# Layer 0's gate product on two float16 parts, with scales taken from the squares of the loaded tiles

## The chip, the cores and the metric

The kernel runs on one core of a Trainium2 chip. The metric is the device time of one execution in microseconds (us). Three runs of the kernel before gave 1795.43 to 1798.64 us, with a median of 1796.76 us.

## The reference

A two-layer transformer block on 256 tokens of width 2048, with a context of 256 more tokens; the widths inside are 4096. Only layer 0, the Fourier branch, matters here. Its input is normalised, scaled and shifted, and its weight matrix gives two halves: `u`, which goes through a Fourier transform and a small mixing product, and `z`, which gates the result.

```python
h = _rmsnorm(x, norm_g[i]) * (1 + scale) + shift      # x and context: 512 columns together
u, z = jnp.split(h @ w_in, 2, axis=-1)                # w_in: 2048 x 8192
...                                                   # u -> Fourier transform, mixing -> f
return f * jax.nn.silu(z)
```

Everything is in float32, and the kernel reaches that accuracy by cutting each operand into a rounded high part and a remainder, with three products for one: high by high, high by low, low by high.

## The kernel before, in words

The program is written as tiles and operations; a planner orders the instructions of each engine by a simulated timeline, by readiness first and by their order in the program after that, and places the waits. `issue_after` lets the author put one instruction behind another on its engine. A pool with a tag holds a fixed number of buffers, and a load waits until one is free.

Layer 0 runs in this order:

- The opening: statistics, the conditioning vectors `gs0` (scale) and `sh0` (shift), and the transform of x.
- The U stage: a loop over 16 groups `g`. Each group loads two raw tiles of 1016 KB (`load_uh`), folds them into a minus part (line 133) and a plus part (line 139 for the first tile; for the second an accumulating DMA from GpSimd's queue, line 142), splits the parts on ScalarE and VectorE (lines 65 and 66) into eight buffers of the pool `wfp`, and multiplies: m-part, then the mixing product of the group before, then p-part. One group takes some 14.4 us in the trace. The raw tiles come from the pool `raw`, with three buffers; the pool `ws` has six of 4 KB.
- The gate stage. `make_hs(k)` makes the 16 moving operands of 128x512: `t = x * gs0 * r_bc` (line 716, VectorE), `h = t + sh0` on ScalarE (line 717), and the remainder on VectorE (line 718), into buffers `act`, of which there are 33. The first four output blocks share four weight tiles `wz0`, all 16 k for four blocks at once (lines 732 to 751). Each of the other 28 blocks (lines 752 to 761) loads one tile `wz` of 1 MB, splits it in two halves, and runs 16 x 3 matmuls of 512 columns (`mm3`, lines 78 to 80). `z_out` takes Silu from PSUM, multiplies it into `y`, and calls `next(ada)`: one piece of the conditioning product of later use, eight multiply-and-sum operations of 128x512 on VectorE (line 687) on another raw tile of 1 MB. There are 31 such pieces in these 28 blocks.
- The output product of layer 0 (lines 798 on) and layer 1 follow.

The weight tiles and the pieces of `ada` share the three raw buffers and the queue of SyncE (SP). Weights and moving operands of the gate product are of type float32r:

```python
    def half_split(t, i):
        h = wsp.tile([P, 1024], F32R, tag="ws", name="wh")
        l = wsp.tile([P, 1024], F32R, tag="ws", name="wl")
        split(h, l, t[:, i * 1024 : (i + 1) * 1024])
        return h, l
...
    us.close()
...
    adat = lay0.enter_context(tc.tile_pool(name="adat", bufs=1))
```

The pool `adat` is opened when the pools of the U stage (`wfp`, `ua`, `up`) have been closed, at the place in SBUF where they began. A pool that lands on a closed pool's bytes waits, by default, for every user of that pool.

Of the kernel before, what the change touches and what calls it, by code (L numbers as in the profile page):

```python
# [3 lines left out]

# [5 lines left out]

# [7 lines left out]
P = 128  # L18
# [13 lines left out]
def tile_dit(ctx: ExitStack, tc: tile.TileContext, a: dict, out: bass.AP):  # L32
# [18 lines left out]

    last_dma = [None]

    def act(dt=F32):
        return actp.tile([P, 512], dt, tag="act", name="act")

    def cload(name, shape, q=None, pool=const):
        t = pool.tile(shape, F32, tag=name, name=name)
# [94 lines left out]

    lay0 = ctx.enter_context(ExitStack())
    adap = lay0.enter_context(tc.tile_pool(name="ada", bufs=1))
    r_bc = adap.tile([P, 512], F32, name="r_bc")
    c32 = adap.tile([P, KT, 32], F32, name="c32")
    GP.memset(c32, 0.0)
# [513 lines left out]
    def ada_jobs():  # L672
        for pieces in ((0,), (1, 2, 3)):
            for kh in range(2):
                cb = adap.tile([P, 2, 1024], F32, tag="cb", name="cb")
                with tc.issue_after(hs_end[2]):
                    nc.gpsimd.dma_start(cb, a["crow"][:, kh].broadcast_to([P, 2, 1024]))
                with tc.issue_after(hs_end[1]):
                    S.activation(cb, cb, AF.Silu)
                for i in pieces:  # L680
                    for fg in range(8):
                        w = raw(a["adw"][i, kh, fg])
# [17 lines left out]
    with tc.tile_pool(name="yp", reuse_waits="tile", bufs=32) as ypool:  # L700
# [4 lines left out]
        hs = []  # L705
        hs_end = [None] * 3

        def make_hs(k):
            xt = act()
            hs_end[2] = nc.gpsimd.dma_start(xt, a["xT"][:, k, :]).ins  # L710
            h, l = act(F32R), act(F32R)
            for s in range(2):
                q = slice(s * N, (s + 1) * N)
                t = xt[:, q]
                with tc.issue_after(ft_end[1]):
                    V.scalar_tensor_tensor(t, t, gs0[:, k, s : s + 1], r_bc[:, q], op0=ALU.mult, op1=ALU.mult)
                hs_end[1] = S.activation(h[:, q], t, AF.Identity, bias=sh0[:, k, s : s + 1]).ins
                hs_end[0] = V.scalar_tensor_tensor(l[:, q], t, sh0[:, k, s : s + 1], h[:, q].bitcast(F32), op0=ALU.add, op1=ALU.subtract).ins
            hs.append((h, l))

        with tc.tile_pool(name="zp", reuse_waits="tile", bufs=2) as zp:
            def z_out(b, o):
                y = ys[b]
                z = zp.tile([P, 512], F32, tag="z", name="z")
                S.activation(z, o, AF.Silu)
                V.tensor_tensor(y, y, z, op=ALU.mult)
                if b >= 4:
                    with tc.issue_after(hs_end[0]) if b < 8 else nullcontext():
                        for _ in range(2 if b in (10, 17, 24) else 1):
                            next(ada)  # L730

            o4 = [psum() for _ in range(4)]
            for kg in range(4):
                wr = raw(a["wz0"][kg])
                w = []
                for i in range(2):
                    make_hs(kg * 4 + i * 2)
                    with tc.issue_after(hs_end[0]) if kg else nullcontext(), tc.issue_after(hs_end[1]) if kg else nullcontext():
                        w.append(half_split(wr, i))
                    make_hs(kg * 4 + i * 2 + 1)  # L740
                for j in range(4):
                    k = kg * 4 + j
                    wh, wl = w[j // 2]
                    for b in range(4):
                        q = slice((j % 2) * 512 + b * P, (j % 2) * 512 + (b + 1) * P)
                        mm3(o4[b], wh[:, q], wl[:, q], hs[k][0], hs[k][1], k == 0, k == KT - 1)
            for b in range(4):
                with tc.issue_after(last_dma[0]):
                    nc.sync.dma_start(ys[b], fd[b])
            for b in range(4):  # L750
                z_out(b, o4[b])
            for b in range(4, NB):
                w = ws_split(raw(a["wz"][b - 4]))
                with tc.issue_after(last_dma[0]):
                    nc.sync.dma_start(ys[b], fd[b])
                o = psum()
                for k in range(KT):
                    wh, wl = w[k // 8]
                    q = slice((k % 8) * P, (k % 8 + 1) * P)
                    mm3(o, wh[:, q], wl[:, q], hs[k][0], hs[k][1], k == 0, k == KT - 1)  # L760
                z_out(b, o)


        x1, sqs = [], []
# [689 lines left out]
```

## Time and profile before

| | |
|---|---|
| median of the runs | 1796.76 us (1795.43 to 1798.64) |
| the profiled execution | 1796.56 us, of which its span is 1794.8 us |
| TensorE (PE) busy | 1759.0 us, 98% of the span |
| VectorE (DVE) busy | 1410.7 us, 79% |
| ScalarE (ACT) busy | 899.5 us, 50% |
| GpSimd (POOL) busy | 211.5 us, 12% |
| granted TensorE clock | 0.998 |
| moved by DMA | 398.86 MB |

PE is the matmul stream and PEld the weight loads beside it. A matmul's duration includes its way through the array, so the rate of a stream is read from the starts of neighbours, not from the durations. An engine's idle time is put down to what ended it.

### The profile page before, as it was taken

The page shows a single profiled execution, that of the slowest core. Times are in us where ns is not written, and L with a number is a line of the kernel's source. Part 1 is how long each engine was busy: PE and PEld are TensorE (multiplying, and loading weights), DVE is VectorE, ACT ScalarE, POOL GpSimd, SP SyncE. Part 2 cuts the span into 40 slices and gives each one's busy share as a digit, 9 for nine tenths or more (in the row PEclk, how much of TensorE's full clock was granted, in tenths as well). Part 3 has the DMA queues.
Part 4 walks back from the last instruction along what each step waited for, and adds up shares of the span by engine and source line. Part 5 has one row for each costly group of instructions (what it writes and reads, how often), then busy time and mean ns, then how long its engine had stood idle before and what let it go on. Part 6 is the DMA issues. An engine that isn't in the chain of part 4 may idle for free. (4 is left out here: it accounts for less than half of the span.)

```text
span 1794.8 us, 26039 instructions
## 1 busy us (share of the span) xinstructions
PE 1759.0 (98%) x9449; PEld 1478.9 (82%) x9449; DVE 1410.7 (79%) x2761; ACT 899.5 (50%) x1543; POOL 211.5 (12%) x213
## 2 busy tenths in 40 slices
PE   6999999999999999999999999999999999999997
PEld 4679999888888888888888888878888888887886
DVE  5779889787879888775986473989999899998455
ACT  5545445432222243323322443678887888886343
POOL 0001112100000000000001000332212211233001
PEclk9999999999999999999999999999999999999999
DMA  9998888666666757662558332488898888887553
GB/s 394 417 344 231 235 231 245 235 219 250 239 231 234 250 194 269 239 238 99 206 200 328 119 120 94 171 187 218 211 211 202 216 211 207 210 211 259 191 185 141
DMA packets 205248, 398.86 MB, mean 222 GB/s; under 512 B 152064, under 2 KB 152464, under 8 KB 170048
## 3 DMA queue, kind: packets, MB, share of 16 engines
q1 hardware_dynamic: 181056, 359.19, 61.9%
q0 software_dynamic: 19920, 31.06, 6.8%
q10 hardware_dynamic: 4144, 6.95, 1.2%
q8 instruction: 74, 1.21, 0.3%
q14 instruction: 54, 0.44, 0.1%
HBM read 352.06 MB, written 12.59 MB: 203 GB/s over the span
## 5 line engine op out<-in xcount | busy, mean ns | idle before, releaser
L65 ACT CAST wh<-raw 128x1024 fp32r<-128x1024 f32 x333 | 348.7, 1049 | 526.6 <-PE ps L79 422.5
L66 DVE TENSOR_TENSOR wl<-raw,wh 128x1024 fp32r<-128x1024 f32 x333 | 426.8, 1286 | 219.4 <-ACT wh L65 216.2
L79 PE MATMUL ps<-act,wh 128*128 128x512 f32 x1024 | 398.2, 389 | 0.0
L78 PE MATMUL ps<-act,wh 128*128 128x512 f32 x1024 | 393.7, 389 | 0.0
L80 PE MATMUL ps<-act,wl 128*128 128x512 f32 x1024 | 392.8, 389 | 0.0
L80 PEld LDWEIGHTS ps<-act,wl 128*128 128x128 f32 x1024 | 192.2, 188 | 39.9
L79 PEld LDWEIGHTS ps<-act,wh 128*128 128x128 f32 x1024 | 192.2, 188 | 39.8
L78 PEld LDWEIGHTS ps<-act,wh 128*128 128x128 f32 x1024 | 192.2, 188 | 39.7
L1119 PE MATMUL ps<-h,wh 128*128 128x512 f32 x512 | 187.1, 403 | 0.0
L687 DVE CUSTOM_DVE_ANT_0 raw<-raw,cb 128x512 f32<-128x512 f32 x256 | 172.6, 688 | 11.2 <-DMA raw<-in_adw 7.6
L687 DVE CUSTOM_DVE_ANT_0 junk<-raw,cb 128x512 f32<-128x512 f32 x192 | 131.9, 687 | 28.6 <-DMA raw<-in_adw 18.0
L1121 PE MATMUL ps<-h,wl 128*128 128x256 f32 x512 | 138.4, 281 | 0.0
L79 PE MATMUL ps<-wl,h 128*128 128x512 f32 x320 | 125.1, 391 | 0.5 <-DVE wl L66 0.5
L80 PE MATMUL ps<-wh,h 128*128 128x512 f32 x320 | 123.8, 390 | 0.0
L78 PE MATMUL ps<-wh,h 128*128 128x512 f32 x320 | 122.4, 397 | 0.0
L1173 DVE SCALAR_TENSOR_TENSOR f<-p,sm,f 128x512 f16<-128x512 f32 x128 | 105.8, 844 | 13.5 <-ACT f L1172 13.3
L1119 PEld LDWEIGHTS ps<-h,wh 128*128 128x128 f32 x512 | 96.5, 188 | 20.7
L1172 ACT ACTIVATE f<-p,sm 128x512 f16<-128x512 f32 x128 | 87.7, 717 | 36.9 <-DMA ft<-f 18.2
L1160 ACT ACTIVATE p<-ps,mx 128x512 f32<-128x512 f32 x128 | 88.0, 689 | 35.1 <-DVE mx L1157 29.6
L1121 PEld LDWEIGHTS ps<-h,wl 128*128 128x128 f32 x512 | 96.9, 189 | 3.0
L1157 DVE CUSTOM_DVE_ANT_0 ps<-ps,mask,nsink 128x512 f32<-128x512 f32 x128 | 93.5, 749 | 0.9 <-PE ps L1156 0.8
L79 PE MATMUL ps<-wl,ys 128*128 128x512 f32 (+1 forms) x192 | 74.1, 386 | 0.1
(339 smaller groups left out, 3375.1 us busy)
## 6 DMA issues: line engine op xcount, KB each, us to landing
raw<-in_wz SPq DMA_DIRECT2D x64, 1024.0 KB, 5.4
raw<-in_adw SPq DMA_DIRECT2D x64, 1024.0 KB, 5.0
raw<-in_awp SPq DMA_DIRECT2D x32, 1024.0 KB, 12.7
raw<-in_wo SPq DMA_DIRECT2D x32, 1024.0 KB, 6.2
raw<-in_wq SPq DMA_DIRECT2D x32, 1024.0 KB, 5.3
raw<-in_wu SPq DMA_DIRECT2D x32, 1016.0 KB, 6.1
raw<-in_wo1b SPq DMA_DIRECT2D x16, 1024.0 KB, 4.9
act<-in_xT POOLq DMA_DIRECT2D x32, 256.0 KB, 6.2
```

Source lines behind the costliest of these rows:

```text
L65: last_cast[0] = S.copy(h, src).ins
L66: last_sub[0] = eng.tensor_tensor(l, src, h.bitcast(F32), op=ALU.subtract).ins
L78: PE.matmul(o, wh, xh, start=start, stop=False)
L79: PE.matmul(o, wh, xl, start=False, stop=False)
L80: return PE.matmul(o, wl, xh, start=False, stop=stop).ins
L687: V.tensor_tensor_reduce(junk if s == 0 and i < 3 else wf, wf, cb[:, s, kq * 512 : kq * 512 + 512], 1.0, 0.0, ALU.mult, ALU.add, acc[:, i, ...
L1119: PE.matmul(o[0], wh[:, q], hx1[k], start=k == 0, stop=k == KT - 1)
L1121: PE.matmul(o[0][:, 0:N], wl[:, q], hx1[k][:, 0:N], start=False, stop=False)
L1157: V.tensor_tensor_reduce(o, o, mask[:, tb, :], -0.125, nsink[:, i : i + 1], ALU.add, ALU.min, mx[:, tb : tb + 1])
L1160: S.activation(pt[tb], so[tb], AF.Exp, bias=mx[:, tb : tb + 1], scale=-1.0, accum_out=sm[:, tb : tb + 1])
L1172: S.activation(f[:, 0:512], pt[tb], AF.Copy, scale=sm[:, tb : tb + 1])
L1173: V.scalar_tensor_tensor(f[:, 512:1024], pt[tb], sm[:, tb : tb + 1], f[:, 0:512], op0=ALU.mult, op1=ALU.subtract)
```

## The change

The gate product's operands become float16 pairs instead of float32r pairs. Since float16 has a narrow range, every weight tile is multiplied by a power of two before it is cut, and the moving operand by another; the result is multiplied back in the scale of the Silu. The power comes from the sum of squares: ScalarE squares the raw tile and sums along the rows, GpSimd sums over the partitions (`partition_all_reduce`), and three VectorE operations on one column turn the exponent into the two factors.

- For the first four blocks the squares are taken in groups 8 to 11 of the U stage, from four loads of `wz0` that are made a second time later; the sum goes through `w4`.
- For the moving operand the squares come from `gs0` and `sh0`; scaled copies of both lie in `hsc`, a tile of `adat`, and `make_hs` reads these.
- For each later block, `fetch(b)` loads the tile, squares it into the buffer that later holds its high part, and makes the factors; it runs two blocks ahead. `split16` then makes both parts in one operation on each engine, 2048 wide, where there were two of 1024.
- Every fourth raw tile of this stage has a buffer of its own (`rawz`), in place of two buffers for `z`, which is now an `act` tile. The 16 moving operands take one `act` buffer each instead of two.

```diff
+    def squares(dump, src, col, scale=1.0):
+        sq_ins[0] = S.activation(dump, src, AF.Square, scale=scale, accum_out=col).ins
+
+    def power(col):
+        tot, e = small("tot"), small("ex", I32)
+        GP.partition_all_reduce(tot, col, P, bass_isa.ReduceOp.add)
+        V.tensor_scalar(e, tot.bitcast(I32), 24, None, op0=ALU.logical_shift_right)
+        return e
+
+    def up_down(e, down):
+        u, d = small("up", bufs=6), small("dn", bufs=6)
+        V.tensor_scalar(u.bitcast(I32), e, -E23, 204 * E23, op0=ALU.mult, op1=ALU.add)
+        V.tensor_scalar(d.bitcast(I32), e, E23, down, op0=ALU.mult, op1=ALU.add)
+        return u, d
+
+    def split16(h, l, src, up):
+        last_cast[0] = S.activation(h, src, AF.Copy, scale=up).ins
+        last_sub[0] = V.scalar_tensor_tensor(l, src, up, h, op0=ALU.mult, op1=ALU.subtract).ins
+
+    def half16():
+        return wsp.tile([P, D], F16, tag="ws", name="w16")
...
+    w4 = adap.tile([P, 4], F32, name="w4")
...
+        if 8 <= g < 12:
+            squares(half16(), raw(a["wz0"][g - 8]), w4[:, g - 8 : g - 7])
...
+        hsc = adat.tile([P, 2, KT, 2], F32, name="hsc")
+        hq = [small("hq") for _ in range(3)]
+        squares(hsc[:, 0], gs0, hq[0], 64.0)
+        squares(hsc[:, 1], sh0, hq[1], 1.5)
+        GP.tensor_tensor(hq[2], hq[0], hq[1], op=ALU.add)
+        eh = power(hq[2])
...
+        V.tensor_scalar(hsc[:, 0], gs0, hup, None, op0=ALU.mult)
+        V.tensor_scalar(hsc[:, 1], sh0, hup, None, op0=ALU.mult)
...
-            h, l = act(F32R), act(F32R)
+            hl = act(F16, 1024)
...
+            def raw4(src):
+                turn[0] += 1
+                if turn[0] % 4:
+                    return raw(src)
+                t = zp.tile([P, D], F32, tag="rawz", name="rawz")
...
+            w1 = small("w1", bufs=1)
+            V.tensor_reduce(w1, w4, axis=AX.X, op=ALU.add)
+            u4, d4 = up_down(power(w1), hdn)
+
+            def fetch(b):
+                t, h, q = raw4(a["wz"][b - 4]), half16(), small("wq")
+                squares(h, t, q)
+                return t, h, *up_down(power(q), hdn)
...
-                        w.append(half_split(wr, i))
+                        split16(wh[:, q], wl[:, q], wr[:, q], u4)
...
-                w = ws_split(raw(a["wz"][b - 4]))
+                t, wh, wu_, wd = nxt.pop(b)
+                wl = half16()
+                split16(wh, wl, t, wu_)
+                if b + 2 < NB:
+                    nxt[b + 2] = fetch(b + 2)
```

More of the change, by code (lines that the diff above doesn't have):

```diff
@@ L6 @@
 import concourse.tile as tile
-from concourse import mybir
+from concourse import bass_isa, mybir
 from concourse._compat import with_exitstack
@@ L52, in tile_dit, with act @@
     last_dma = [None]
-    def act(dt=F32):
-        return actp.tile([P, 512], dt, tag="act", name="act")
+    def act(dt=F32, n=512):
+        return actp.tile([P, n], dt, tag="act", name="act")
     def cload(name, shape, q=None, pool=const):
@@ L155, in tile_dit, with small @@
     adap = lay0.enter_context(tc.tile_pool(name="ada", bufs=1))
+    E23 = float(1 << 23)
+    BIG = 2.0**15
+    def small(tag, dt=F32, bufs=4):
+        return adap.tile([P, 1], dt, tag=tag, name=tag, bufs=bufs)
+    def squares(dump, src, col, scale=1.0):
[10 more added lines that the diff above has]
+        return u, d
+    sq_ins = [None]
+    def split16(h, l, src, up):
[3 more added lines that the diff above has]
+        return wsp.tile([P, D], F16, tag="ws", name="w16")
     r_bc = adap.tile([P, 512], F32, name="r_bc")
@@ L681, in ada_jobs @@
                     for fg in range(8):
-                        w = raw(a["adw"][i, kh, fg])
+                        w = ada_raw(a["adw"][i, kh, fg])
                         for f in range(2):
@@ L757, in tile_dit @@
                 for k in range(KT):
[L758 to L759 removed]
+                    q = slice(k * P, (k + 1) * P)
                     mm3(o, wh[:, q], wl[:, q], hs[k][0], hs[k][1], k == 0, k == KT - 1)
[L761 removed]
+                z_out(b, o, wd)
+        ada_raw = raw
         x1, sqs = [], []
```

36 lines of the change are left out of this document (22 added, 14 removed).

## The prediction

> **What bounds the kernel now.** I read the page first, then the stretches of the gate stage, then the starts of neighbouring matmuls in the timeline, then the groups that the change touches, and at the end SP's queue and the seam between U stage and gate stage.
>
> ```profile
> span 1794.8 us, 26039 instructions
> PE 1759.0 (98%) x9449; PEld 1478.9 (82%) x9449; DVE 1410.7 (79%) x2761; ACT 899.5 (50%) x1543; POOL 211.5 (12%) x213
> ...
> 322.00:366.00 44.00, 44.00 (x201) 36.65 (x200) 35.53 (x72) 23.17 (x42) 3.22 (x6) 1.00 0.60 210
> 367.00:672.00 305.00, 305.00 (x1347) 252.57 (x1346) 250.74 (x600) 85.90 (x102) 1.06 (x2) 1.00 0.62 230
> ```
>
> The last two rows are the gate stage: its first four blocks, then the 28 others. The columns are the stretch's length, then busy PE, weight loads, DVE, ACT, POOL, then granted clock, DMA share and GB/s. PE is busy for the whole of both, at clock 1.00, so only faster matmuls can shorten it, and any wait brought in lengthens it. DVE is second: 35.53 / 44 = 81% and 250.74 / 305 = 82%.
>
> The rate of a matmul stream is read from starts:
>
> ```profile
> 278.91 0.28 PE L78 MATMUL ps<-act,wmh 128*127 128x256 f32 x1
> ...
> 284.54 0.28 PE L80 MATMUL ps<-act,wml 128*127 128x256 f32 x1
> ...
> 380.33 0.39 PE L78 MATMUL ps<-act,wh 128*128 128x512 f32 x1
> ...
> 384.41 0.39 PE L78 MATMUL ps<-act,wh 128*128 128x512 f32 x1
> ...
> 1310.82 0.27 PE L1190 MATMUL ps<-ft,v 128*128 128x256 f16 x1
> ...
> 1311.58 0.27 PE L1191 MATMUL ps<-ft,v 128*128 128x256 f16 x1
> ```
>
> Between the first two lie 47 steps: 5.63 / 47 = 119.8 ns for 256 float32r columns. Between the next two lie 18: 4.08 / 18 = 226.7 ns for 512. Between the last two lie 7: 0.76 / 7 = 108.6 ns for 256 float16 columns, with new weights for each matmul as in the gate product.
>
> **The change, part by part.**
>
> *The matmuls.* From 256 to 512 columns float32r pays 226.7 - 119.8 = 106.9 ns. No row shows 512 float16 columns; if those 256 further columns cost the same, it is 108.6 + 106.9 = 215.5 ns, 11.2 ns less. The stage has 32 blocks x 16 k x 3 = 1536 matmuls: 1536 x 11.2 ns = 17.2 us. The ends: nothing, if at 512 columns something else sets the pitch, and 21.2 ns each (32.5 us), if float16 gains in proportion, 226.7 x 108.6 / 119.8 = 205.5. I take 17.2, since the 106.9 is measured between two streams that differ in nothing but width. PE then needs 48 x 215.5 ns = 10.34 us for a block, where it needs 10.88 now.
>
> *VectorE in the 28 blocks.*
>
> ```profile
> L66 DVE TENSOR_TENSOR wl<-raw,wh x333: 1196/1224/2322, 305.0 to 1772.4; 128x1024 fp32r<-128x1024 f32 x167
> ...
> L1173 DVE SCALAR_TENSOR_TENSOR f<-p,sm,f x128: 735/747/3701, 1163.0 to 1632.4; 128x512 f16<-128x512 f32 x128
> ...
> L718 DVE SCALAR_TENSOR_TENSOR act<-act,sh x32: 476/483/488, 311.1 to 363.9; 128x256 fp32r<-128x256 f32 x32
> ...
> L1294 DVE TENSOR_SCALAR s<-s 128x1 f32<-128x1 f32 x2 | 0.3, 154 | 0.1
> ```
>
> Out go two remainders of 1224 ns, 2.45 us. In comes one scaled remainder of 2048 columns: from 483 ns at 256 and 747 at 512 it is 1.03 ns a column, so 747 + 1536 x 1.03 = 2.33 us. Three one-column operations of 154 ns add 0.46. DVE now works 82.2% of 10.88 = 8.94 us a block; it will work 8.94 - 2.45 + 2.33 + 0.46 = 9.28 us of 10.34, or 90%. PE's work still hides it, but the cover is down to 1.06 us a block. In the first four blocks the operations stay the same in number, 35.53 us of what becomes 192 x 215.5 ns = 41.4: 86%.
>
> *ScalarE.* Out go two casts, in come a square with its row sum and a scaled copy:
>
> ```profile
> L65 ACT CAST wh<-raw 128x1024 fp32r<-128x1024 f32 x333 | 348.7, 1049 | 526.6 <-PE ps L79 422.5
> ```
> ```profile
> L182 ACT ACTIVATE dump<-xn x4: 1905/1910/1911, 6.3 to 15.2; 128x2048 f32<-128x2048 f32 x4
> L182 ACT ACTIVATION_READ_ACCUMULATOR dump<-xn x4: 185/186/186, 8.1 to 17.0; 128x1 f32 x4
> ```
>
> The square is 1.91 + 0.19 us, and the copy takes about as long. That is 2 x 1.91 + 0.19 - 2 x 1.05 = 1.9 us more a block on an engine that is 85.90 / 305 = 28% busy: nothing.
>
> *GpSimd's sum.* No row shows a sum over partitions. Near it on POOL are these, and the loads' times to landing:
>
> ```profile
> L1296 POOL TENSOR_TENSOR fv<-ss,s x2: 191/191/191, 1779.9 to 1787.4; 128x1 f32<-128x1 f32 x2
> ...
> L1262 POOL TENSOR_TENSOR act<-act,fg 128x512 f32<-128x512 f32 x6 | 12.0, 2031 | 105.2 <-ACT act L1260 105.2
> ...
> DMA to landing us min/median/max: 6.6/7.6/11.1
> ```
> ```profile
> raw<-in_wz SPq DMA_DIRECT2D x64, 1024.0 KB, 5.4
> ...
> raw<-in_wu SPq DMA_DIRECT2D x32, 1016.0 KB, 6.1
> ```
>
> The third row is the accumulating DMA of line 142, the one job of POOL's queue here that crosses memory. So 0.2 us from below and 7.6 from above; I take 2.0, by the longest operation that POOL itself carries out, since a sum over 128 partitions is more than a sum within them and needs no memory outside. In the 28 blocks it runs two blocks ahead. The tile has 2 x 10.34 = 20.7 us from the release of its buffer to its first matmul. It needs 5.4 us for the load, 2.1 for the square, 2.0 for the sum, 0.5 for the factors, 1.9 for the copy and 2.3 for the remainder: 14.2 us, so the sum is hidden from PE. What it can hold up is DVE: behind the shift that waits for it stand the remainder of the next block and eight operations of `ada`. I allow 0.1 us of PE waiting a block: 3 us.
>
> The Trainium skill's "GPSIMD Engine Reference" (2.1 Instruction dispatch) says that the first call of a freshly loaded kernel on those cores pays some 6 us for its code. No run here shows it; if that fell on the seam described next, the sum would end 6 us higher, an estimate by that page.
>
> *The seam.* `hsc` lies in `adat`, on the bytes of `wfp`. The last reader of `wfp` is the last product of the U stage:
>
> ```profile
> 319.48 0.88 DVE L716 SCALAR_TENSOR_TENSOR act<-act,gs,r_bc 128x256 f32<-128x256 f32 x2 [5.28 <-DMA act<-in_xT]
> ...
> 320.55 0.88 DVE L718 SCALAR_TENSOR_TENSOR act<-act,sh 128x256 fp32r<-128x256 f32 x2 [0.18 <-ACT act L717]
> ...
> 321.02 0.29 PE L80 MATMUL ps<-act,wpl 128*127 128x260 f32 x1
> ...
> 321.99 0.39 PE L78 MATMUL ps<-act,wh 128*128 128x512 f32 x1
> ...
> 326.38 0.39 PE L80 MATMUL ps<-act,wl 128*128 128x512 f32 x1
> ```
> ```profile
> L124 ACT ACTIVATE cc<-cc x1: 229/229/229, 3.0 to 3.0; 128x32 f32<-128x32 f32 x1
> ```
>
> Today the first moving operand is ready before 321.02, so PE goes from the U stage into the gate product at 321.99, with the last mixing product among it. Now the chain starts at 321.3 (the end of 321.02): two small squares with their sums, 2 x (0.23 + 0.19) = 0.8; POOL's add 0.2; the sum 2.0; five small DVE operations, 0.8; then an operand (319.48 to its high part's end takes 1.4). The gate product starts near 326.5. By 326.38 PE has today done the mixing product and 14 gate matmuls (3.2 us); then it will have done the mixing only. Loss: 3.3 us, with handovers 3.5. At the ends of POOL's price it is 1.7 and 9.1; if `hsc` does not wait, nothing.
>
> *The U stage.* Groups 8 to 11 each gain a load, a square (2.1 us on ACT) and the use of a raw buffer.
>
> ```profile
> 206.00:221.00 15.00, 15.00 (x127) 15.00 (x126) 13.18 (x20) 6.99 (x14) 2.60 (x3) 1.00 0.89 242
> ...
> 219.40 0.33 SPq L49 DMA_DIRECT2D raw<-in_wu  x1
> 225.57 0.33 SPq L49 DMA_DIRECT2D raw<-in_wu  x1
> 234.20 0.33 SPq L49 DMA_DIRECT2D raw<-in_wu  x1
> ...
> 293.40 0.28 PE L78 MATMUL ps<-act,wmh 128*127 128x256 f32 x1
> ```
>
> A group takes 14.5 us: from 278.91, the first matmul of one m-part, to 293.40, that of the next. Its two tiles pass through three buffers, each load at the moment when one is free, so releases lie 6.2 and 8.6 us apart in turn. The extra tile holds a buffer for load and square, 6.1 + 2.1 = 8.2 us, and fits in the longer gap; one tile of each group is then loaded 8.6 us later. DVE is 13.18 / 15 = 88% busy there, so I put 1.5 us for order. The second loads of `wz0` lie in place of the present ones: nothing.
>
> *Sum.* 1796.6 (the profiled execution, 1.8 us above its span, 0.2 below the median) - 17.2 + 3.0 + 3.5 + 1.5 = 1787.4 us. Later stages stay PE's, and `z` in an `act` buffer and the 16 buffers freed there only loosen waits: nothing.
>
> **The rivals.**
>
> *DVE waits for POOL in each block (slower).* If the planner thinks the sum shorter than it is, the shift stands at the head of DVE's queue too early, by s, every block. Above s = 1.06 DVE sets the pace: block = 9.28 + s. With s = 2.0, the sum's whole assumed time, it is 11.28, 0.94 over PE: 28 x 0.94 = 26.3 us in place of the 3.0, 1810.7 us. The gain is gone from s = 1.06 + 12.2 / 28 = 1.5. For it: 90% DVE, and an engine that takes its work in order. Against: two blocks of lead, by which a well placed shift never waits. A sum near 7.6 us that the planner doesn't know would give s over 3 and over 1835.
>
> *The U stage is held by its buffers (no change).* If the extra tile takes its buffers in strict turn, the second tile of a group must be freed before the next one loads: load 6.1 + fold 1.2 (priced as line 66) + accumulating DMA 7.6 + cast and remainder 2.3 = 17.2, where a group takes 14.5. Four groups lose 10.8, less some 2 that PE may have in hand: 1787.4 - 1.5 + 8.8 = 1794.7. Against: loads go to whichever buffer is free.
>
> *The narrower type gains nothing at 512 columns.* Then 1796.6 + 8.0 = 1804.6; the float16 rows speak against it.
>
> *The pitch falls far.* Then DVE sets the pace at 9.28 us: 28 x (10.88 - 9.28) = 44.8 us, and 44 - 35.5 = 8.5 in the first blocks, 1796.6 - 53.3 + 5.0 = 1748.3. Against: 108.6 ns at half the width leaves no room for less than that at 512. The Trainium skill's "TensorE: Matmul & The Clock Gate" (Back-to-back issue gap) has a sustained 131 ns for 512 columns. The trace does not bear that out: its float16 stream takes 108.6 ns for 256.
>
> **How the numbers follow.** The three runs lie 0.18% apart, so 0.2% (3.6 us) is about what can be told from no change. Chances: the forecast 0.53, the far pitch 0.02; held buffers or an eaten gain 0.11; DVE behind POOL 0.26, no gain at 512 columns 0.03, a seam with the sum at its upper price and other waits 0.05. So faster 0.55, same 0.11, slower 0.34. The forecast's own range is 1779.4 (no new waits) to 1793. The range reaches up past DVE's case at s = 2.0 and leaves out its worse half and the far pitch: 1779 to 1815.
>
> **What would show it.** Right: gate matmuls 215 ns apart, PE over 97% busy from the fifth block on, DVE near 90%, a PE gap of 3 to 5 us behind the last U product, groups 9 to 12 still 14.5 us long. Wrong: one-column operations on DVE with long waits on POOL; gate matmuls with gaps on the remainder of line 66's successor; POOL's sum over 4 us; a pitch of 227.

## The result, and the profile after

Four runs of the changed kernel gave 1820.12 to 1828.83 us, median 1823.35; four of the kernel before on the same chip 1795.43 to 1799.03, median 1797.70. The ratio is 1.0147, with a 95% interval of 1.012 to 1.0174: slower by 1.5%. The profiled execution took 1820.12 us (span 1818.3), where 1787.4 was forecast.

The page's head, and the stretches of the changed kernel: four of the U stage, the two of the gate stage (its first four blocks, then the 28 others), and the 15 us after the gate stage. Columns as in the prediction.

```profile
span 1818.3 us, 26147 instructions
PE 1753.6 (96%) x9449; PEld 1345.3 (74%) x9449; DVE 1418.8 (78%) x2826; ACT 960.3 (53%) x1583; POOL 228.2 (13%) x244
...
225.00:240.00 15.00, 11.26 (x87) 11.04 (x86) 10.30 (x16) 7.89 (x13) 2.56 (x3) 0.92 0.81 269
240.00:255.00 15.00, 15.00 (x122) 14.94 (x121) 11.50 (x18) 6.82 (x12) 2.02 (x2) 0.96 0.80 223
255.00:270.00 15.00, 13.66 (x113) 13.44 (x112) 10.97 (x16) 6.13 (x13) 1.27 (x4) 1.00 0.89 287
270.00:285.00 15.00, 12.97 (x95) 12.97 (x96) 12.31 (x18) 7.75 (x12) 2.45 (x3) 0.89 0.77 206
344.00:388.00 44.00, 43.42 (x188) 18.98 (x188) 36.30 (x74) 28.74 (x45) 4.88 (x10) 0.93 0.66 246
389.00:684.00 295.00, 290.37 (x1342) 130.42 (x1341) 253.00 (x643) 126.29 (x112) 13.70 (x27) 1.00 0.64 236
685.00:700.00 15.00, 7.21 (x17) 5.13 (x17) 9.77 (x22) 10.13 (x19) 0.00 (x0) 0.72 0.58 210
```

Before the change PE was full in all of these places. Now all but one (240 to 255) have holes, and the granted clock is down in them or behind them (0.92, 0.96, 0.89, 0.93, 0.72), so that a hole costs more than its own length.

Where the 23.5 us of span went is read from the first and the last matmul of each stage (start, plus duration for an end). In the kernel before, the gate stage and the output stage look alike; the last gate matmul is the 1536th of this form, counted from 321.99 (the starts are evenly spaced, so no record is missing):

```profile
671.15 0.39 PE L80 MATMUL ps<-act,wl 128*128 128x512 f32 x1
```

| us | before | after | difference | forecast |
|---|---|---|---|---|
| end of the last U matmul ahead of the gate stage | 322.2 | 333.6 | +11.5 | +1.5 |
| from there to the first gate matmul | -0.2 | 10.5 | +10.7 | +3.5 |
| gate stage, first matmul to the end of the last | 349.5 | 340.8 | -8.7 | -14.2 |
| from there to the end of the span | 1123.3 | 1133.3 | +10.1 | 0 |
| span | 1794.8 | 1818.3 | +23.5 | -9.2 |

In the kernel before, ten matmuls of the last mixing product, some 1.2 us, run among the gate's; in the changed kernel all of it runs ahead of the seam. So of the first difference 1.2 us belong to the third. Counted to the last product of a p-part (321.3 before, 331.6 after), the U stage ends 10.3 us later.

**The pitch.** Two rows of the timeline, 21 matmuls apart, show what the change was made of:

```profile
671.91 0.38 PE L78 MATMUL ps<-act,w 128*128 128x512 f16 x1
...
676.44 0.38 PE L78 MATMUL ps<-act,w 128*128 128x512 f16 x1
```

4.53 / 21 = 215.7 ns, where 215.5 was forecast. The Trainium skill's "TensorE: Matmul & The Clock Gate" (Wait — 56ns, not 53.3ns?) gives the same 215.7 ns start to start for 512 columns on a busy array. The 131 ns of its later section, which the prediction names, is borne out by no run here.

**The U stage.** SP's queue, VectorE, ScalarE and PE around two of the extra loads (those of `in_wz`):

```profile
209.65 0.33 SPq L49 DMA_DIRECT2D raw<-in_wz  x1
218.99 3.88 SPq L49 DMA_DIRECT2D raw<-in_wu  x2
229.70 0.33 SPq L49 DMA_DIRECT2D raw<-in_wz  x1
...
227.33 1.22 DVE L133 TENSOR_TENSOR wm<-raw 128x1016 f32<-128x1016 f32 x1 [2.10 <-DMA raw<-in_wu]
...
234.58 1.91 ACT L163 ACTIVATE w<-raw 128x2048 f16<-128x2048 f32 x1 [0.27 <-DMA raw<-in_wz]
...
236.40 0.19 ACT L163 ACTIVATION_READ_ACCUMULATOR w<-raw 128x1 f32 x1
236.49 1.02 ACT L65 CAST wmh<-wm 128x1016 fp32r<-128x1016 f32 x1
237.42 0.61 ACT L65 CAST mh<-mt 128x512 fp32r<-128x512 f32 x1
...
238.09 0.58 PE L78 MATMUL ps<-mh,ch 128*128 128x256 f32 x1 [3.74 <-ACT mh L65]
```

The extra tile holds one of three buffers, the group's own load is issued late, VectorE's fold waits for it, and on ScalarE the square, the late cast of a weight part and the small cast that PE waits for stand one behind the other. That small cast, of `mh`, ran at 229.07 in the kernel before. Of the 8.4 us by which it is late, 1.9 are ScalarE's queue: VectorE had made its input by 235.50. PE waits for such a cast 8.0 us in three waits, of which one of 0.9, at 88 us, is there before the change too. Of the groups, the four that start from 219.8 on take 18.3, 15.9, 18.1 and 16.0 us instead of 14.4.

**The seam.**

```profile
331.31 0.29 PE L80 MATMUL ps<-act,wpl 128*127 128x260 f32 x1
...
332.52 0.19 POOL L745 TENSOR_TENSOR hq<-hq 128x1 f32<-128x1 f32 x1 [17.25 <-ACT hsc L163]
...
338.30 0.40 POOL L167 PARTITION_ALL_REDUCE tot<-hq  x1 [5.58 <-issue]
...
341.14 2.19 ACT L180 ACTIVATE w<-raw,up 128x1024 f16<-128x1024 f32 x2 [0.46 <-DVE dn L174]
...
343.24 0.89 ACT L762 ACTIVATE act<-act,hsc 128x256 f16<-128x256 f32 x2
344.18 1.86 PE L78 MATMUL ps<-act,w 128*128 128x512 f16 x4 [10.54 <-ACT act L762]
```
```profile
L167 POOLq MODIFY_POOL_CONFIG  x2: 11/11/11, 332.7 to 332.7; - x2
```

Between GpSimd's addition and its first partition sum lie 5.58 us in which it waits for nothing that the trace shows, right behind a MODIFY_POOL_CONFIG. I take this for the load of the sum's code. The Trainium skill's "GPSIMD Engine Reference" (2.1 Instruction dispatch) gives some 6 us for the first call of a freshly loaded kernel; the trace's 5.58 agrees. ScalarE then makes two weight splits (2.19 us) ahead of the operand.

**The gate stage** by groups: the chain square, sum, exponent, split.

```profile
L163 ACT ACTIVATE w<-raw 128x2048 f16<-128x2048 f32 x26 | 49.6, 1908 | 71.7 <-DMA raw<-in_wz 71.7
L167 POOL PARTITION_ALL_REDUCE tot<-wq x28 | 13.7, 490 | 271.5 <-ACT w L163 245.0 <-DVE acc L720 26.5
L168 DVE TENSOR_SCALAR ex<-tot 128x1 int32<-128x1 int32 x30 | 4.6, 152 | 26.9 <-POOL tot L167 26.9
L180 ACT ACTIVATE w<-raw,up 128x2048 f16<-128x2048 f32 (+1 forms) x28 | 50.6, 1813 | 37.4 <-DVE up L173 37.0 <-DVE dn L174 0.5
L181 DVE SCALAR_TENSOR_TENSOR w<-raw,up,w 128x2048 f16<-128x2048 f32 (+1 forms) x28 | 59.2, 2119 | 3.1 <-ACT w L180 3.1
```

The sum itself takes 0.49 us in the mean, but VectorE waits 26.9 us for it (6.3 of them at the seam), because the sum waits for the square and the square for the load. In one block, for example, the load is issued at 478.53, the square starts at 483.48, when the tile has landed, and the sum at 485.57; VectorE's shift follows at 485.99 after a wait of 0.44 us. The remainder of the block before comes behind it, at 487.62.

**The end of the gate stage.**

```profile
686.63 0.68 ACT L782 ACTIVATE act<-ps,dn 128x512 f32<-128x512 f32 x1
...
687.39 8.41 ACT L65 CAST act<-y 128x512 fp32r<-128x512 f32 x16
```
```profile
691.51 0.69 DVE L720 CUSTOM_DVE_ANT_0 raw<-raw,cb 128x512 f32<-128x512 f32 x1 [3.81 <-DMA raw<-in_adw]
...
695.70 1.89 DVE L66 TENSOR_TENSOR act<-y,act 128x512 fp32r<-128x512 f32 x3
```
```profile
688.07 3.63 PE L78 MATMUL ps<-act,wh 128*128 128x512 f32 x8 [3.05 <-ACT act L65]
696.44 0.80 PE L79 MATMUL ps<-act,wh 128*128 128x512 f32 x1 [4.74 <-DVE act L66]
```

All 16 first casts of the output stage's operand run behind the last silu. The kernel before had 13 of them ahead of it, at 672.82 (one expectation below says twelve):

```profile
661.91 3.26 ACT L65 CAST act<-y 128x512 fp32r<-128x512 f32 x6
...
666.86 3.23 ACT L65 CAST act<-y 128x512 fp32r<-128x512 f32 x6
...
672.30 0.62 ACT L65 CAST act<-y 128x512 fp32r<-128x512 f32 x1
672.82 0.59 ACT L725 ACTIVATE z<-ps 128x512 f32<-128x512 f32 x1
```

Their remainders on VectorE stand behind a piece of `ada` that waits 3.81 us for its load. PE is empty for 3.05 us, then for 4.74, and the stretch has a clock of 0.72.

### The profile page after: what moved, and what is told of

Same layout as the page of the kernel before. It is cut to its first block, busy times and chain, and to the rows that moved or that the text cites. A ratio compares the mean times of both kernels' runs of the same rounds, so it can differ in the third digit from the quotient of the medians.

```text
span 1818.3 us, 26147 instructions
## 1 busy us (share of the span) xinstructions
PE 1753.6 (96%) x9449; PEld 1345.3 (74%) x9449; DVE 1418.8 (78%) x2826; ACT 960.3 (53%) x1583; POOL 228.2 (13%) x244
## 5 line engine op out<-in xcount | busy, mean ns | idle before, releaser
L65 ACT CAST wh<-raw 128x1024 fp32r<-128x1024 f32 x269 | 281.2, 1046 | 369.8 <-PE ps L79 303.6
L66 DVE TENSOR_TENSOR wl<-raw,wh 128x1024 fp32r<-128x1024 f32 x269 | 349.1, 1302 | 155.9 <-ACT wh L65 153.4
L79 PE MATMUL ps<-act,wh 128*128 128x512 f32 x512 | 200.4, 391 | 4.7 <-DVE act L66 4.7
L78 PE MATMUL ps<-act,wh 128*128 128x512 f32 x512 | 199.6, 395 | 3.0 <-ACT act L65 3.0
L78 PE MATMUL ps<-act,w 128*128 128x512 f16 x512 | 189.8, 381 | 10.5 <-ACT act L762 10.5
L80 PE MATMUL ps<-act,wl 128*128 128x512 f32 x512 | 198.0, 391 | 0.0
L80 PE MATMUL ps<-act,w 128*128 128x512 f16 x512 | 191.9, 381 | 4.6 <-DVE w L181 4.3
L79 PE MATMUL ps<-act,w 128*128 128x512 f16 x512 | 194.4, 381 | 0.4 <-DVE act L763 0.4
L720 DVE CUSTOM_DVE_ANT_0 raw<-raw,cb 128x512 f32<-128x512 f32 x224 | 150.7, 689 | 30.0 <-DMA raw<-in_adw 26.7
L720 DVE CUSTOM_DVE_ANT_0 junk<-raw,cb 128x512 f32<-128x512 f32 x160 | 110.0, 687 | 37.0 <-DMA raw<-in_adw 23.4
L79 PEld LDWEIGHTS ps<-act,wh 128*128 128x128 f32 x512 | 96.8, 189 | 25.4 <-DVE act L66 5.5
L78 PEld LDWEIGHTS ps<-act,wh 128*128 128x128 f32 x512 | 97.5, 191 | 24.0 <-ACT act L65 3.5
L1244 DVE SCALAR_TENSOR_TENSOR f<-p,sm,f 128x512 f16<-128x512 f32 x128 | 104.8, 836 | 11.5 <-ACT f L1243 11.1
L80 PEld LDWEIGHTS ps<-act,wl 128*128 128x128 f32 x512 | 96.8, 189 | 20.3
```

The costliest lines, as they stand in the source:

```text
L65: last_cast[0] = S.copy(h, src).ins
L66: last_sub[0] = eng.tensor_tensor(l, src, h.bitcast(F32), op=ALU.subtract).ins
L78: PE.matmul(o, wh, xh, start=start, stop=False)
L79: PE.matmul(o, wh, xl, start=False, stop=False)
L80: return PE.matmul(o, wl, xh, start=False, stop=stop).ins
L1244: V.scalar_tensor_tensor(f[:, 512:1024], pt[tb], sm[:, tb : tb + 1], f[:, 0:512], op0=ALU.mult, op1=ALU.subtract)
```

## The experiments

Four losses, four suspects: the extra loads in the U stage, the seam's chain with its code load, the order of the small operations on VectorE, and the queue at the end of the gate stage. Each kernel is compared with runs of the kernel before on the same chip; the changed kernel's ratio was 1.0147.

**An early partition sum** (against the changed kernel):

```diff
     GP.memset(mhalf, -0.5)
+    warm = const.tile([P, 1], F32, name="warm")
+    GP.partition_all_reduce(warm, ones, P, bass_isa.ReduceOp.add)
```

> One more partition sum, of a constant column, is issued on GpSimd in the opening, before the U stage; nothing else is changed. In the changed kernel the first partition sum began 5.58 us after the addition in front of it, behind a MODIFY_POOL_CONFIG, and the first gate matmul came 12.9 us after the last U matmul. Theory A (these 5.6 us are the first call's code load, and they lie on the path): the sum follows its addition within 0.5 us, the seam falls from 12.9 to 7 to 8 us, the time from 1823 to about 1818. Rival B (the seam is held by the pool of the scaled vectors, which opens only when the U stage's operands are gone, and by the two splits that stand ahead of the operand in ScalarE's queue): the wait for the code goes but the seam stays above 11 us and the time at 1822 to 1824.

Measured: 1835.64 us, 1.0216 (1.0201 to 1.0231), 12 us slower. Neither theory had this. GpSimd's timeline, with the row of the seam last:

```profile
13.20 0.40 POOL L107 PARTITION_ALL_REDUCE warm<-consts  x1 [11.15 <-issue]
23.52 0.59 POOL L91 TENSOR_TENSOR r0r<-r0v,consts 128x1 f32<-128x1 f32 x1 [9.92 <-issue]
...
352.94 0.40 POOL L169 PARTITION_ALL_REDUCE tot<-hq  x1 [5.89 <-issue]
```
```profile
L91 POOLq MODIFY_POOL_CONFIG  x4: 37/60/83, 13.6 to 1022.7; - x4
```

The code is not loaded once and for all. The powers of line 91 seem to belong to other code, since they now have a MODIFY_POOL_CONFIG of their own ahead of them: going to the sum costs 11.15 us, going back to the power 9.92, and at the seam it is paid again, 5.89. The opening waits for these powers, and the first matmul moved from 11.3 to 26.1 us. The seam stayed at 10.9. That the load alone holds the seam was neither shown nor excluded here.

**No extra loads in the U stage:**

```diff
-        if 8 <= g < 12:
-            squares(half16(), raw(a["wz0"][g - 8]), w4[:, g - 8 : g - 7])
+    GP.memset(w4, 1.0)
```

> Left out: the extra load of the first four blocks' weights in groups 8 to 11 of the U stage and the squares of them; their column is set to 1.0, so that the factor of those blocks is a constant. Theory A (the extra load takes a raw buffer from the U stage's own loads, the late fold puts its casts ahead of the evacuation cast in ScalarE's queue, and the matmul engine idles): the last U matmul, at 321.0 in the kernel before and 331.3 in the changed one, comes back to 321 to 322.5, the waits of the matmul engine on the cast of mh (7.1 us in all) fall under 1 us, and the time falls by about 10 us, to 1813. Rival B (the U stage is late because of the clock, not the loads): the last U matmul stays after 328 and the time above 1820.

Measured: 1811.62 us, 1.0081 (1.0064 to 1.0098). The last U matmul ends at 323.1 instead of 333.6, and PE's waits on the cast of `mh` are 0.9 us instead of 8.0. Theory A holds: 10.6 us are these loads with their squares, which left together, and the rest of the 11.5 is the mixing product that now runs ahead of the seam. The seam (10.6) and the gate stage (342.8) did not get shorter.

**No sums per tile:**

```diff
-                t, h, q = raw4(a["wz"][b - 4]), half16(), small("wq")
-                squares(h, t, q)
-                return t, h, *up_down(power(q), hdn)
+                t, h = raw4(a["wz"][b - 4]), half16()
+                return t, h, u4, d4
```

> Left out: the squares, the partition sum and the three small operations of each of the 28 later blocks; all blocks are split by the factor of the first four. The loads, the scaled split and the seam stay. Theory A (VectorE loses about 1 us per block to the chain square, sum, exponent, and the remainders come late): the gate stage, 340.8 us from first matmul to last, falls to 331 to 334, the waits of matmuls and weight loads on the remainder (12.8 us in all) fall under 3 us, the time falls by 7 to 10 us, and to more if the casts at the start of the output stage come earlier too. Rival B (it is VectorE's own work, the 2048-wide scaled remainder of 2 us beside the adaptation pieces, that makes the remainders late): the gate stage stays above 338 and the time within 3 us of 1823.

Measured: 1813.66 us, 1.0091 (1.0076 to 1.0106). The gate stage takes 335.0 us instead of 340.8, and no matmul or weight load waits for the remainder. So the 2048-wide remainder is not what holds PE; the chain for the sum is. The 335.0 us are still 3.7 more than 1536 x 215.7 ns = 331.3; most of them lie behind the seam, where the first four blocks have a granted clock of 0.93, as in the changed kernel. The loss at the end of the gate stage stayed (1132.3 us from there to the end).

**The pair alone**, that is the two edits above, the early sum, and `hsc` in the pool `ada`, open all along, instead of `adat`:

> All at once: no extra load and no squares in the U stage, no squares and sums per block (both replaced by constants), the scaled vectors of the operand in a pool that is open all along so that their sum can run during the U stage, and a first partition sum in the opening. What is left of the change is the float16 pair with its scaled split. Theory A (the pair is worth its matmul pitch, 1536 times 11 us/1000, and everything lost is lost to the scales): the last U matmul at 321 to 322, a seam of at most 4 us, a gate stage of 331 to 334 us, and a time of 1780 to 1788, below the kernel before. Rival B (the scaled split, one 2048-wide remainder on VectorE where there were two of 1024, and a cast of 2 us on ScalarE, holds the stage by itself): the gate stage above 337 us and a time of 1793 or more.

Measured: 1808.92 us, 1.0064 (1.0049 to 1.0079). The seam is gone (the first gate matmul starts among those of the last mixing product, as in the kernel before), and the gate stage takes 333.7 us, 15.8 less than before the change. The rest was spent elsewhere: 14.6 us on the early sum in the opening, and 1131.6 us behind the gate stage instead of 1123.3. A's stages were right, its total wrong, since two losses were not in my list.

**`hsc` in the open pool, alone:**

```diff
-        hsc = adat.tile([P, 2, KT, 2], F32, name="hsc")
+        hsc = adap.tile([P, 2, KT, 2], F32, name="hsc")
```

> One line of the changed kernel: the scaled vectors of the operand (hsc) lie in the pool that is open from the start, not in the one that opens when the U stage's operands are gone. Nothing else. Theory A (the seam of 10.8 us is the chain of squares, addition, code load of 5.6 us, sum, exponent and two splits, and it begins only when the U stage's operand pool is free): the chain runs during the U stage, the first gate matmul comes within 1 us of the last U matmul, and the time falls from 1823 to about 1813. Rival B (the code load takes GpSimd away from the accumulating loads of the U stage, or the factor of the first four blocks, whose squares come in group 11, holds the seam by itself): the seam stays above 5 us or the U stage grows by as much, and the time stays above 1819.

Measured: 1819.10 us, 1.0115 (1.010 to 1.0131). Both theories are half right: the seam is gone, and the U stage ends 5.9 us later than in the changed kernel, by the last product of a p-part (337.5 against 331.6). VectorE shows why, between the opening and the U stage:

```profile
125.71 0.16 DVE L168 TENSOR_SCALAR ex<-tot 128x1 int32<-128x1 int32 x1 [4.20 <-POOL tot L167]
...
131.96 0.42 DVE L658 TENSOR_TENSOR asp<-ps,asp 32x260 fp32r<-32x260 f32 x1
```
```profile
PE ps L679 <- DVE asp L658: 3.7, 1, 3.7
```

The exponent stands in VectorE's queue during the code load, an evacuation stands behind it, and PE waits for that. Not the loads of GpSimd, as B had it, but VectorE's order.

**The silu in PSUM:**

```diff
-                z = act()
-                S.activation(z, o, AF.Silu, scale=dn)
-                V.tensor_tensor(y, y, z, op=ALU.mult)
+                S.activation(o, o, AF.Silu, scale=dn)
+                V.tensor_tensor(y, y, o, op=ALU.mult)
```

> One edit of the changed kernel: the silu of a gate block is written back to its PSUM tile, so that no tile of it is taken from the ring of 33 operand tiles; the kernel before took it from a pool of its own. Theory A (since the silu's tile comes from the operand ring, all sixteen first casts of the output stage's operand stand in ScalarE's queue behind the last silu, where the kernel before had twelve ahead of it; this empties the matmul engine at the start of the output stage for about 10 us, and no experiment so far has mended it): eight or more of these casts run before the last gate matmul ends, the 15 us that begin with that end hold 60 or more matmuls instead of 17, and the time falls from 1823 to about 1814. Rival B (the output stage starts late because the weight tiles are loaded late, their buffers being held by late adaptation pieces): the casts come earlier but the matmuls wait for the weights, and the time stays above 1820.

Measured: 1823.10 us, 1.0131 (1.0106 to 1.0156). The profiled execution took 1814.98, with eight casts ahead of the last silu and 51 matmuls in the first 15 us instead of 17; the other three took 1822.7 to 1825.1. In the profiled execution 1130.1 us follow the gate stage, 3.2 less than in the changed kernel. Inconclusive: the order changed as A said, and the time did not follow.

**The small operations later:**

```diff
-                return t, h, *up_down(power(q), hdn)
+                return t, h, total(q)
...
-                t, wh, wu_, wd = nxt.pop(b)
+                t, wh, tot = nxt.pop(b)
+                with tc.issue_after(last_sub[0]):
+                    wu_, wd = up_down(power(None, tot), hdn)
```

`total` is the partition sum without the exponent.

> Only the order on VectorE is changed: the three small operations on a block's sum are issued when the block's split is due, behind the remainder of the block before, instead of when its weights are asked for, two blocks ahead. The loads, squares and sums stay where they are. Theory A (VectorE, which works in order, stands about 1 us per block at the first of them, for a load, a square and a sum that come last, and that makes the remainders late): its waits for the sum, 26.9 us in 22 waits with 6.3 of them at the seam, fall under 10, the gate stage falls from 340.8 us to 333 to 335, the time from 1823 to about 1817. Rival B (ScalarE's squares, 1.9 us for each block in front of the cast of an earlier one, make the casts late and with them the remainders): VectorE's waits move to the cast and the gate stage stays above 338 us.

Measured: 1814.03 us, 1.0082 (1.0065 to 1.0099). VectorE's waits for the sum fall from 26.9 us to 9.2, of which 6.4 at the seam; the gate stage takes 336.0 us. Theory A holds: with all squares and sums still there, 4.9 of the 5.8 us that leaving them out gave come from the order alone. The profiled execution is the slowest of the four (1816.81 us), and its U stage, which the edit does not touch, ends 2.8 us later than in the changed kernel; why is not shown.

**The pair without the early sum, with the silu in PSUM:**

> The kernel with all four parts at once that cost 1808.9 us, less its early sum (which moved the first matmul of the kernel from 11.2 to 25.8 us, since the code was loaded before the opening's powers and again after), and with the silu written to PSUM. Left out, as there: the squares and sums of the weights; constants stand in their place. Theory A (the opening lost 14.6 us to the early sum and the start of the output stage about 10 us to the queue): 1808.9 - 14.6 - 9.7 = 1784.6, range 1781 to 1789, that is 0.4 to 0.9 per cent under the kernel before: the float16 pair is worth its 17 us of matmul pitch less a few. Rival B (part of the 10 us at the start of the output stage is the late weight loads): 1790 to 1795. Rival C (the first sum's code load, now at 120 us, stops the U stage's loads): the last U matmul after 328 and the time above 1795.

Measured: 1793.65 us (1788.52 to 1798.15), 0.9979 (0.9965 to 0.9992); 1788.52 in the profiled execution. The opening's 14.6 us came back and 1125.2 us follow the gate stage, but the U stage ended 5.5 us later than before the change. VectorE stood 3.84 us for the code load and PE 3.9 for the evacuation, the wait just shown. None of the three theories had it.

**All mended.** Against the changed kernel:

```diff
-        hsc = adat.tile(...)
+        hsc = adap.tile(...)
+        with tc.issue_after(evacs[6][1]):
+            eh = power(hq[2])
...
+                z = zp.tile([P, 512], F32, tag="z", name="z", bufs=1)
...
-            V.tensor_reduce(w1, w4, axis=AX.X, op=ALU.add)
+            wr0 = raw4(a["wz0"][0])
+            wh0 = half16()
+            squares(wh0, wr0, w1, 2.0)
...
+                with tc.issue_after(last_sub[0]):
+                    wu_, wd = up_down(power(None, tot), hdn)
```

> The change with four mends: the operand's scaled vectors in the open pool, with VectorE's part of their chain ordered behind the evacuation of group 6 (in the runs before, VectorE stood 3.84 us for the code load at 120 us, with an evacuation of the opening behind it, and the U stage ended 4.6 us late); the small operations on a block's sum behind the remainder of the block before; the silu's tile from a pool of its own (the adaptation's dump is float16, to make room); and no extra load in the U stage: the factor of the first four blocks comes from the squares of their first weight tile, times four, out of the tile that is split anyway. Left out: the squares of the other three tiles of these blocks. All other factors are from data, as in the change. Theory A (the four losses were independent, and this removes the 10.6 us of the U stage, the 10.7 of the seam, 5 to 7 of the gate stage and 6 to 10 at the start of the output stage): 1823.4 - 10.6 - 10.7 - 5 - 8 = 1789, range 1785 to 1793, under the kernel before. Rival B (they overlap, one wait taking another's place: the square of the first tile at the end of the U stage, or adaptation pieces that come late): 1795 to 1805.

Measured: 1780.77 us (1778.74 to 1784.30), 0.991 (0.9897 to 0.9922): 0.9% under the kernel before, 2.3% under the changed one, and better than theory A's range. The stretches of the gate stage, and the 15 us behind it:

```profile
322.00:366.00 44.00, 44.00 (x210) 20.77 (x209) 34.90 (x74) 28.57 (x45) 3.15 (x7) 1.00 0.60 223
367.00:654.00 287.00, 286.99 (x1330) 129.92 (x1329) 253.89 (x649) 134.51 (x126) 25.21 (x27) 1.00 0.66 243
655.00:670.00 15.00, 15.00 (x68) 12.41 (x67) 13.57 (x32) 4.79 (x6) 0.00 (x0) 1.00 0.58 211
```
```profile
679.19 0.50 PE L80 MATMUL ps<-act,wl 128*128 128x512 f32 x1 [2.36 <-DVE wl L66]
```

PE is full again in these stretches. One hole is left behind them, at 679, where PE waits 2.36 us for a remainder of the output stage's weights; the kernel before has none there. The last U matmul ends at 321.6, the gate stage takes 333.1 us with all 28 sums in it, and 1124.4 us follow. The code load is still there, at 118.8 us, but nothing on VectorE stands behind it. Of the pitch's 17.2 us, 15.8 reach the span (1794.8 - 1779.0).

**The pair with the same order, sums replaced by constants:**

> The float16 pair with constants in place of the weights' squares and sums (left out, as before), the operand's scaled vectors early with VectorE's part behind the evacuation of group 6, and the silu's tile in its own pool. Against the kernel of 1793.7 us it differs in the order of that chain and in the place of the silu. Theory A (VectorE's wait for the code load of the first sum cost the U stage 4.6 us and the slow clock after it): the last U matmul comes at 322 to 324 instead of 327.7 and the time falls by 4 to 6 us, to 1788 to 1790; the whole is then what the pair can give here, the pitch of 17 us less what is late elsewhere. Rival B (the last U matmul is late for the loads): it stays after 326 and the time at 1793.

Measured: 1789.71 us, 0.9957 (0.9944 to 0.997). The last U matmul ends at 322.6, so the wait for the code load was the cause of the 5 us there: theory A. Odd is that this kernel, with less to do, is 9 us slower than the one above, 5.6 us by the spans of the two profiled executions. 4.0 of these lie behind the gate stage (1128.4 us against 1124.4). PE waits there, up to 760 us, in four holes of 4.8 us together for casts and remainders of the output stage's weights, against 2.6 us in two holes in the kernel above; what makes these late was not settled.

**The silu's line in the kernel before**, where `z = zp.tile(...)` becomes `z = act()` and nothing else:

> The kernel before with one line changed: the silu's tile is taken from the ring of operand tiles, as the change does it. Everything else is the kernel before, float32 parts and no sums. Theory A (it is this line that puts the output stage's first casts behind the last silu on ScalarE and empties the matmul engine there): the U stage and the gate stage stay (last gate matmul at about 672.8), the 15 us behind it hold 45 or fewer matmuls instead of 68, and the time rises from 1797 to 1803 to 1807. Rival B (the gap needs the late loads of the changed kernel too): the matmul engine stays full and the time within 2 us of 1797.

Measured: 1799.64 us, 1.0014 (1.0005 to 1.0022): 2 us, not 6 to 10 (4.3 by the spans of the two profiled executions). The casts of `y` do move behind the last silu, but the output stage is short of its operand for 2.1 us only; 56 matmuls run in the 15 us instead of 68. VectorE's remainders find no late piece of `ada` ahead of them there. My theory had the place right and the price wrong.

**The same line in the mended kernel:**

```diff
-                z = zp.tile([P, 512], F32, tag="z", name="z", bufs=1)
+                z = act()
```

> The kernel of 1780.8 us with one of its mends undone: the silu's tile is taken from the ring of operand tiles again (and the adaptation's dump is float32 again). Left out, as there: the squares of three of the first four blocks' four tiles. In the kernel before this line alone cost 2.1 us, not the 6 to 10 that I had put down to it. Theory A (its price depends on what VectorE has in front of it: with the float16 pair the adaptation's passes wait for late loads at the end of the gate stage, and the casts that come in one batch behind the last silu then find the remainders queued behind those passes): the 30 us behind the last gate matmul hold 95 to 110 matmuls instead of 117, and the time rises by 4 to 7 us, to 1785 to 1788. Rival B (the line costs 2 us everywhere, and the rest of the 10 us belonged to VectorE's waits for the sums): 1782 to 1784, at least 112 matmuls.

Measured: 1788.19 us, 0.9952 (0.994 to 0.9964): 7.4 us for this line together with the dump's type: theory A, a little beyond its range (93 matmuls in the 30 us instead of 117). The stretch, and ScalarE and VectorE in it:

```profile
655.00:670.00 15.00, 8.63 (x25) 6.55 (x26) 9.72 (x25) 9.54 (x19) 0.00 (x0) 0.77 0.55 204
```
```profile
656.11 8.43 ACT L65 CAST act<-y 128x512 fp32r<-128x512 f32 x16
```
```profile
658.55 0.69 DVE L721 CUSTOM_DVE_ANT_0 raw<-raw,cb 128x512 f32<-128x512 f32 x1 [2.53 <-DMA raw<-in_adw]
...
662.75 0.68 DVE L66 TENSOR_TENSOR act<-y,act 128x512 fp32r<-128x512 f32 x1
```

It is the picture of the changed kernel: one batch of casts behind the last silu, the remainders behind a piece of `ada` that waits for its load, 25 matmuls where there were 68, and a clock of 0.77. The start and the end of the gate stage are those of the mended kernel within 0.2 us.

## Why the prediction was wrong, point by point

- **The matmuls: right.** 215.7 ns against 215.5, and a gate stage of 333.1 to 333.7 us where nothing holds it, 15.8 to 16.4 us shorter where 17.2 was worked out.
- **The durations: right.** The remainder takes 2.35 us (2.33), the three small operations 0.50 (0.46), the square 1.91 + 0.19, the copy 2.00. GpSimd's sum takes 0.38 us in the median, where I took 2.0 between ends of 0.2 and 7.6.
- **VectorE in the 28 blocks: mechanism right, size wrong.** I allowed 3.0 us. The stage took 340.8 us where 1536 x 215.7 ns are 331.3, so 9.5 were lost: 5.8 to the sums of the blocks, by the run that leaves them out, and 3.7 that this run still has, most of them behind the seam at a lower clock. "Two blocks of lead, by which a well placed shift never waits" was the sentence that failed: the planner placed the shift where the load and the square were not done, and VectorE stood 20.6 / 28 = 0.7 us a block at it. This is my first rival with a smaller s, and through the load instead of the sum. The point from which it costs, 1.06 us of spare, was a mean; PE lost already at 0.7, presumably since the waits do not fall evenly.
- **The seam: place right, size wrong.** 3.5 us forecast, 10.7 found. By the trace the partition sum with its code load took 5.58 + 0.40 = 5.98 us where the forecast had 2.0, which is 4.0 of the missing 7.2. I had the code load, in a sentence beside the sum, with its 6 us; the sum itself left it out because no row of the trace before had it. The two splits of 2.19 us ahead of the operand on ScalarE, which the chain did not have at all, are the next part; and VectorE does four other operations (338.91 to 340.44) between the exponent and the scaling of the operand's vectors. How these share the rest no run shows.
- **The U stage: the wrong case chosen.** "Fits in the longer gap" failed. The loads came one after another through the three buffers, as in my second rival, which priced the loss at 8.8 us; 10.6 were measured when the loads and their squares were taken out. I counted when a buffer is free, but not ScalarE, on which the late cast stands ahead of a cast that PE needs, nor the clock after a hole.
- **"Later stages stay PE's, and `z` in an `act` buffer [...] only loosen waits: nothing": wrong**, by 10.1 us. Taking the silu's tile from the operand's ring puts the next stage's casts behind the last silu, which fits a planner that gives out a ring's tiles in the order of the program. That line costs 7.4 us in the mended kernel (with the dump's type) and 2.1 in the kernel before. I saw a pool with more room and did not ask who takes the next tile from it.

So the gain was real and stayed real; it was lost in four places that each stand at the edge of a stage or in a queue. The changed kernel has the pair's 17 us and loses about 40: some 30 to the loads, the chain and the order of the scales (10.3 in the U stage, 10.5 at the seam, 9.5 in the gate stage), and 10 behind the gate stage, where the silu's tile has its part. In the mended kernel, with other orders and without three of the first four squares, 15.8 of the 17.2 reach the span.

What stays open: why the kernel without sums is slower than the mended one; and why the silu in PSUM, with the changed kernel's other losses in place, gained in one run of four only. That the mended kernel with all four squares of the first blocks would be as fast was not tried.

## What to carry to other kernels

A chain that runs "two blocks ahead" is hidden only if nothing stands behind its waiting instructions: look at each engine's queue, and put the instruction that waits behind the work that is due before it. When PE is 98% busy, price the stage edges first, that is what the first operand of the next stage waits for, and which pool its tiles come from. Here the partition sum on GpSimd had to be counted with a code load each time GpSimd changed over to it, and the power too when it came behind the sum in the opening.

## What the runs showed of the hardware

- In these runs GpSimd paid anew for the code when it changed between the power and the partition sum: 5.6 to 7.1 us on the way to the sum in the later stages, and 11.2 to the sum and 9.9 back to the power in the opening, where the page shows 340 GB/s and more. The sum of one column over 128 partitions itself takes 0.38 us.
- A matmul of 512 columns starts every 215.7 ns in float16 and every 226.7 in float32r. The difference of 11 ns is the same at 256 columns (108.6 and 119.8), so at these two widths float32r costs the same time more per matmul.
- Stretches of 15 us in which holes of 3 to 5 us in PE's stream ended had a granted clock of 0.72 to 0.92. At the start of the output stage matmuls of 512 columns started 427 ns apart behind the hole (697.04 to 701.30), where 227 is usual.
